# F and H projections as 2x2 block products in one list with the gates and the last projection

## The chip, the cores and the metric

The kernel runs on one core of a Trainium2 chip. The time is the device time of that core in microseconds (us), and lower is better. Before the change the median of three runs is 2470.0 us (2466.16 to 2470.41).

## What is computed

One encoder layer is applied to two sequences (batch 0 and 1) of 1024 positions with 1024 channels, all in float32. Cut to what matters here:

```python
xn = rmsnorm(x, g_pre)
p = xn @ w_in                                   # 8 sections of 1024 columns
fv, fg, hv, hg, mg = jnp.split(p, ...)
fz = jnp.fft.fftn(fv grouped, axes=(1, 3)).real # Fourier branch
y_f = (fz * jax.nn.silu(fg)) @ w_fourier_out    # the F projection
z = two long convolutions of short_conv(hv)     # Hyena branch
y_h = (z * jax.nn.silu(hg)) @ w_hyena_out       # the H projection
g_f, g_h = jnp.split(jax.nn.sigmoid(mg + b_merge), 2, axis=-1)
out = (g_f * y_f + g_h * y_h) @ w_out           # the last projection
return x + rmsnorm(out, g_post)
```

## The kernel before

Every product in float32 is made of three matmuls. A number is split into a rounded high part and the rest, both in a type that the tensor engine takes (fp32r), and `mm3` (line 369) adds high x high, high x low and low x high in one PSUM bank. `split` (line 168) is the pair of instructions that makes the parts: ACT casts the high part, and DVE (or POOL) subtracts it from the source. PE only ever sees tiles of 128x128 against 128x512.

The kernel has four phases. `phase_fourier` and `phase_main` make the Fourier branch, the filters, both convolutions and most of the gate sections; the change does not touch them. `phase_gates` and `phase_out` come last, and they are replaced.

`phase_gates` (line 971) makes the last ten pairs of gate sections of batch 1. A pair is 256 output channels by 1024 positions. It is computed as a 2x2 block product with seven multiplications in place of eight: weights and operand are cut in four blocks each, sums of blocks are formed, and `times` (line 954) runs 12 matmuls for each of seven products. `prepare` (line 981) loads the 1 MB of weights of a pair on POOL's queue, makes the sums of its blocks on DVE and splits seven operands. The operand (xn of batch 1, transposed) and the sums of its blocks are made once before the list and stay in SBUF. `first` runs the products 11 and 12 of the next pair ahead of the products s4 and 22 of the running one; `out` (line 1025) takes the four results out of PSUM, and multiplies those of two sections by a tile that it loads.

`phase_out` (line 1082) makes F and H in four units (batch, half of the positions). In a unit there are eight output tiles of F and eight of H, each of 24 matmuls of full width (`project`, line 1120): no block products. The weights of each tile are loaded on POOL's queue (`weight`, line 1106) and split, and since a unit has half of the positions they are loaded and split twice per batch. The operand of the next unit is loaded and split tile by tile beside the running one (`operand`, `rounded`, `ahead`). `gated` (line 1138) loads the merge gate, applies the sigmoid and multiplies. F stays in SBUF until H of the same tile is there, the two are added on DVE, and the sum is written to DRAM tensors `d_m`. Beside this, `beside` (line 1152) loads the last weights w_out and makes their block sums; two of the four sums are kept in DRAM (`d_t`) for a while.

`last_rows` (line 1238) makes the last projection as a list of eight pairs with the same seven products as the gates: the rows of `d_m` are the weights' side, w_out and its sums are the operand. `half_row` and `finish` do the row norm and write y.

The order of the instructions on each engine is set by a planner at compile time, from the order of the program and its own estimate of times; the queues of all engines, those of the transfers among them (SP's and POOL's), are then worked off in that order. `tc.issue_after` and `keep_in_program_order` hold single instructions back or in place.

Of the kernel before, what the change touches and what calls it, by code (L numbers as in the profile page):

```python
# [16 lines left out]
P = 128  # L17
D = 1024
# [143 lines left out]
class K:  # L162
# [34 lines left out]
    def setup(self, ctx):  # L197
# [29 lines left out]
        self.d_m = [dt(f"d_m{u}", [P, 4, 8, P]) for u in range(2 * NB)]  # L227
        self.d_t = [dt(f"d_t{j}", [P, 4, 512]) for j in range(2)]
# [734 lines left out]
    def sums(self, s, r):  # L963

        self.sub("dve", s[:, 0::2], r[:, 0:2], r[:, 1::2])
        self.stt("dve", s[:, 1], s[:, 0], -1.0, r[:, 3], MUL, SUB)
        self.add("dve", s[:, 3], s[:, 1], r[:, 2])

    PLAIN = [(5, 0), (5, 1), (6, 0), (6, 1), (5, 2), (5, 3), (6, 2), (6, 3), (5, 4), (5, 5), (6, 4), (6, 5)]

    def phase_gates(self):
# [4 lines left out]
        wp, b = self.wp, 1  # L976
        jobs = [(s, c) for c in range(0, 8, 2) for s in (0, 4, 5, 6) if (s, c) not in self.PLAIN]
        with ExitStack() as es:
            pool = lambda n: es.enter_context(tc.tile_pool(name=n, bufs=1, reuse_waits="tile"))
            gs, gw, gr = pool("gs"), pool("gw"), pool("gr")  # L980
            def prepare(sec, c):


                r = gr.tile([P, 4, 512], F32, tag="raw", name="wraw", bufs=2)
                for i in range(2):
                    nc.gpsimd.dma_start(r[:, 2 * i:2 * i + 2].rearrange("p a b -> p (a b)"), a["w_in"][sec, c + i])
                s = gw.tile([P, 4, 512], F32, tag="sum", name="wsum", bufs=1)
                A = {}

                def parts(n, pool, tags, src, bufs):  # L990
                    h, l = [pool.tile([P, 4, P], F32R, tag=t, name=t, bufs=bufs) for t in tags]
                    self.split(h.rearrange("p a b -> p (a b)"), l.rearrange("p a b -> p (a b)"), src, "dve", "act")
                    A[n] = h, l
                parts("11", wp, ("wh", "wl"), r[:, 0], 2)
                parts("12", wp, ("wh", "wl"), r[:, 1], 2)
                self.add("dve", s[:, 0:2], r[:, 2].unsqueeze(1).to_broadcast([P, 2, 512]), r[:, 3::-3])
                self.add("dve", s[:, 2], s[:, 0], r[:, 0])
# [5 lines left out]
                self.add("dve", s[:, 3], s[:, 2], r[:, 1])  # L1003
# [4 lines left out]
            A = prepare(*jobs[0])  # L1008
            TH, TL = [], []
            for k in range(4):  # L1010
                r = gr.tile([P, 4, 512], F32, tag="raw", name="xraw", bufs=2)
                for i in range(2):
                    nc.sync.dma_start(r[:, 2 * i:2 * i + 2].rearrange("p a b -> p (a b)"), self.d_x[b][k + 4 * i])
                s = gw.tile([P, 4, 512], F32, tag="sum", name="xsum", bufs=1)
                self.sums(s, r)
                h, l = [gs.tile([P, 4, 512], F32R, tag=f"{t}{k}", name=f"{t}{k}", bufs=1) for t in ("th", "tl")]
# [421 lines left out]
```

## Time and profile before

| | us |
|---|---|
| median of three runs | 2470.0 |
| lowest and highest run | 2466.16, 2470.41 |
| span of the profiled execution (first to last instruction) | 2468.1 |
| PE busy in it | 2408.3 |
| DVE busy | 1947.5 |
| ACT busy | 1093.3 |
| POOL busy | 498.2 |

The time of the profiled execution as a whole is not printed on the page; the span is what its instructions take. The page gives the busy time of each engine, and views of the trace give it for stretches of the span: PE multiplies, PEld loads PE's weights, DVE and ACT work on tiles, POOL works on tiles and issues some transfers, SP issues the others. A row of a group of instructions has the source line, the engine, the operation, output and inputs by name, their shapes, the count, busy time, the mean of one in ns, and the idle time of the engine ahead of them with what ended it. Since `split`, `tt` and `mm` are helpers, most rows carry one of their lines (171, 177, 181, 194), and the tile names tell them apart: `pin` are the products of the input projections, `pg` those of `phase_gates`, `pyf` and `pyh` those of F and H, `po` those of the last projection.

### The profile page before, as it was taken

How to read it: one execution, taken by the hardware profiler on the slowest of the kernel's cores; microseconds unless marked ns; L12 is line 12 of the kernel's file. 1: busy time of each engine (PE TensorE's matmuls, PEld its weight loads, DVE VectorE, ACT ScalarE, POOL GpSimd, SP SyncE). 2: the span in 40 equal slices, each digit the busy share in tenths (PEclk: the TensorE clock that was granted, in tenths of full speed). 3: DMA queues.
4: the chain of work that ended last, by engine and by line, in shares of the span. 5: the costliest groups of instructions: out<-in, count | busy, mean ns of one | idle time of the engine just before them, and what ended most of it. 6: DMA issues, size and time to landing. Idle time of an engine off the chain costs nothing.

```text
span 2468.1 us, 37202 instructions
## 1 busy us (share of the span) xinstructions
PE 2408.3 (98%) x13196; PEld 2090.7 (85%) x13196; DVE 1947.5 (79%) x3725; ACT 1093.3 (44%) x2041; POOL 498.2 (20%) x516
## 2 busy tenths in 40 slices
PE   6999999999989999999999999999999999999998
PEld 6988888888878988888889888888788888888886
DVE  7687788888888999999889999985565455665677
ACT  5546666666654333334223222333343444544443
POOL 1331222212234333442000000112200012112121
PEclk9999999999999999999999999999999999999999
DMA  7535544444556455545443443435445567776543
GB/s 272 180 128 210 206 163 151 156 160 156 169 184 201 161 176 175 162 161 199 137 145 129 137 144 131 136 129 175 154 162 173 196 201 267 246 244 221 165 168 128
DMA packets 225155, 429.39 MB, mean 174 GB/s; under 512 B 23542, under 2 KB 87255, under 8 KB 224456
## 3 DMA queue, kind: packets, MB, share of 16 engines
q1 hardware_dynamic: 198444, 333.34, 40.6%
q0 software_dynamic: 26336, 93.65, 10.8%
q8 instruction: 104, 1.70, 0.3%
q14 instruction: 83, 0.68, 0.1%
q10 hardware_dynamic: 188, 0.02, 0.0%
HBM read 290.60 MB, written 136.31 MB: 173 GB/s over the span
## 4 chain that ended last, share of the span: by engine, by line
PE 55%; DMA 2%; issue 1%; DVE 1%; POOL 0%; ACT 0%; DVEq 0%; SPq 0%; ACTq 0%; POOLq 0%
PE pin L194 20%; PE pg L194 8%; PE po L194 6%; PE pT L194 6%; PE pyh L194 5%; PE pX L194 5%; PE pyf L194 5%; DMA wr<-in_w_fo 1%; PE tph L785 1%; DMA g<-d_g 1%; DMA wr<-in_w_ho 0%; DVE wl L181 0%; POOL wr L1113 0%; ACT wh L171 0%; POOL wl L181 0%
## 5 line engine op out<-in xcount | busy, mean ns | idle before, releaser
L194 PE MATMUL pin<-xh,wh 128*128 128x512 f32 x1472 | 578.2, 394 | 4.3 <-DVE v L177 2.9
L194 PE MATMUL pin<-xh,wl 128*128 128x512 f32 x1472 | 577.1, 393 | 2.5 <-POOL wl L181 2.5
L194 PE MATMUL pin<-xl,wh 128*128 128x512 f32 x1472 | 578.4, 393 | 0.0
L181 POOL TENSOR_TENSOR wl<-wr,wh 128x512 fp32r<-128x512 f32 x136 | 253.5, 1865 | 1162.8 <-ACT wh L171 1120.3
L194 PEld LDWEIGHTS pin<-xh,wh 128*128 128x128 f32 x1472 | 278.4, 189 | 55.6 <-DVE v L177 3.1
L194 PEld LDWEIGHTS pin<-xh,wl 128*128 128x128 f32 x1472 | 278.3, 189 | 54.0 <-POOL wl L181 3.4
L194 PEld LDWEIGHTS pin<-xl,wh 128*128 128x128 f32 x1472 | 278.5, 189 | 51.5 <-DVE xl L181 0.4
L171 ACT CAST wh<-wr 128x512 fp32r<-128x512 f32 x264 | 162.7, 618 | 304.3 <-PE pin L194 106.8
L194 PE MATMUL pT<-cinv,yh 128*128 128x256 f32 x1024 | 192.1, 282 | 0.0
L194 PEld LDWEIGHTS pT<-cinv,yh 128*128 128x128 f32 x1024 | 164.8, 190 | 9.5 <-ACT yh L171 0.2
L181 DVE TENSOR_TENSOR t<-pX,k 128x1024 f32<-128x1024 f32 x128 | 155.4, 1214 | 9.7 <-PE pX L194 8.7
L181 DVE TENSOR_TENSOR wl<-wr,wh 128x512 fp32r<-128x512 f32 x128 | 87.1, 687 | 92.6 <-ACT wh L171 92.3
L194 PE MATMUL pX<-bh,cfwd 128*128 128x256 f32 x768 | 160.1, 287 | 0.0
L194 PE MATMUL pyf<-sf,wh 128*128 128x512 f32 x512 | 157.7, 389 | 0.0
L194 PE MATMUL pyh<-sh,wh 128*128 128x512 f32 x512 | 157.2, 389 | 0.0
L171 ACT CAST yh<-y 128x512 fp32r<-128x512 f32 x128 | 79.5, 621 | 153.7 <-DVE y L181 120.6
L194 PE MATMUL pT<-cinv,yl 128*128 128x256 f32 x512 | 144.9, 283 | 1.2 <-DVE yl L181 1.2
L171 ACT CAST bh<-b 128x512 fp32r<-128x512 f32 x144 | 88.6, 619 | 119.9 <-DVE b L181 81.5
L181 DVE TENSOR_TENSOR bl<-b,bh 128x512 fp32r<-128x512 f32 x144 | 110.6, 769 | 23.4 <-ACT bh L171 23.4
L194 PEld LDWEIGHTS pX<-bh,cfwd 128*128 128x128 f32 x768 | 125.5, 190 | 3.0
L194 PEld LDWEIGHTS pyf<-sf,wh 128*128 128x128 f32 x512 | 96.0, 188 | 20.3 <-ACT wh L171 0.5
L194 PEld LDWEIGHTS pyh<-sh,wh 128*128 128x128 f32 x512 | 96.1, 188 | 20.0
(350 smaller groups left out, 5322.9 us busy)
## 6 DMA issues: line engine op xcount, KB each, us to landing
k<-d_k SPq DMA_DIRECT2D x128, 512.0 KB, 4.0
wr<-in_w_in SPq DMA_DIRECT2D x136, 256.0 KB, 3.1
d_g<-gt SPq DMA_DIRECT2D x124, 256.0 KB, 2.5
d_k<-kt SPq DMA_DIRECT2D x128, 128.0 KB, 2.2
d_k<-kt SPq DMA_DIRECT2D x64, 256.0 KB, 2.3
wr<-in_w_fo POOLq DMA_DIRECT2D x64, 256.0 KB, 3.9
g<-d_g SPq DMA_DIRECT2D x64, 256.0 KB, 3.8
wr<-in_w_ho POOLq DMA_DIRECT2D x64, 256.0 KB, 3.8
```

The costliest lines, as they stand in the source:

```text
L171: self.rounded = nc.scalar.copy(h, src)
L181: return e.tensor_tensor(out, a, b, op=op)
L194: return self.nc.tensor.matmul(out, lhsT, rhs, start=start, stop=stop, skip_group_check=shared)
L785: nc.tensor.transpose(tp[:, q * P:(q + 1) * P], eo[:, e, q], self.ident)
```

## The change

F and H become jobs of the same list as the gates and the last projection. The new `phase_blocks` replaces `phase_gates`, `phase_out` and `last_rows`. The list is: ten gate pairs, four pairs each of F and H of batch 0, four each of F and H of batch 1, and eight pairs of the last projection. Each job has seven products of 12 matmuls. Six operands follow each other: xn of batch 1, the F operand and the H operand of batch 0, those of batch 1, and w_out.

What is new around the products:

- `staged` makes the four block sums of a coming operand on POOL, a quarter at a time: two loads on SP's queue, three POOL operations, and one store of 1 MB to `d_t` on POOL's queue. For w_out it also copies the rows to `d_wo`. It runs beside the gate jobs 1 to 8 (operands 1 and 2), the jobs 10 to 17 (operands 3 and 4) and 18 to 21 (w_out).
- Where the operand changes (the last job of each group), `room` loads and splits the blocks 00, 10 and 11 of the new operand, and `sum_of` loads and splits the four sums.
- The sums of the weights' blocks in `prepare` are on POOL for F and H, and on DVE otherwise.
- `out` of an F job writes the gated result to `d_m`; that of an H job adds its result to `d_m` in DRAM by an accumulating store on POOL's queue. `d_m` is now laid out by channel tiles, and the load for the last projection picks 128 columns of each.
- The weights of F and H are loaded and split once for each batch.
- The area for POOL's transfer descriptors is set to 8192.

The core of the diff (`last_rows` goes on as `open_row`, `half_row` and `finish` with little change):

```diff
-    def phase_gates(self):
-    def phase_out(self):
-    def last_rows(self, units, B11, B21, B22, T1, T2, T3, T4, gp, op):
+    def phase_blocks(self):
...
+        jobs = [("x", s, c) for c in range(0, 8, 2) for s in (0, 4, 5, 6) if (s, c) not in self.PLAIN]
+        for q in range(4):
+            jobs += [("fh"[q % 2], q // 2, c) for c in range(0, 8, 2)]
+        jobs += [("o", u, t) for u in range(4) for t in (0, 2)]
+        nx = len(jobs) - 24
+        operand = [0] * nx + [1 + q // 4 for q in range(16)] + [5] * 8
...
             def prepare(i):
                 kind, x, c = jobs[i]
                 r = gr.tile([P, 4, 512], F32, tag="raw", name="wraw", bufs=2)
+                for j in range(2):
+                    out = r[:, 2 * j:2 * j + 2].rearrange("p a b -> p (a b)")
+                    if kind == "o":
+                        nc.gpsimd.dma_start(out.rearrange("p (k c) -> p k c", k=8), self.d_m[x][:, :, P * (c + j):P * (c + j) + P])
+                    else:
+                        nc.gpsimd.dma_start(out, a["w_in"][x, c + j] if kind == "x" else a[f"w_{kind}o"][c + j])
                 s = gw.tile([P, 4, 512], F32, tag="sum", name="wsum", bufs=1)
+                eng = "pool" if kind in "fh" else "dve"
...
+                self.add(eng, s[:, 0:2], r[:, 2].unsqueeze(1).to_broadcast([P, 2, 512]), r[:, 3::-3])
+                self.add(eng, s[:, 2], s[:, 0], r[:, 0])
...
+                self.add(eng, s[:, 3], s[:, 2], r[:, 1])
...
+            def staged(q, k):
+                src = source(q)
+                r = ga.tile([P, 4, 512], F32, tag="draw", name="draw", bufs=1)
+                for i in range(2):
+                    nc.sync.dma_start(f2(r[:, 2 * i:2 * i + 2]), src(k + 4 * i) if q < 5 else a["w_out"][(k + 4 * i) * P:(k + 4 * i + 1) * P])
+                    if q == 5:
+                        nc.gpsimd.dma_start(src(k + 4 * i), f2(r[:, 2 * i:2 * i + 2]))
+                s = ga.tile([P, 4, 512], F32, tag="dsum", name="dsum", bufs=1)
+                self.sub("pool", s[:, 0::2], r[:, 0:2], r[:, 1::2])
+                self.sub("pool", s[:, 1], s[:, 2], r[:, 0])
+                self.add("pool", s[:, 3], s[:, 1], r[:, 2])
+                nc.gpsimd.dma_start(self.d_t[q][:, k], s)
+
+            def room(q, i, n):
+                out = []
+                for k in range(4):
+                    t = xp.tile([P, 2, 512], F32R, tag=f"x{'hl'[i - n]}{k + 4 * n}", name=f"b{i}{n}{k}", bufs=1)
+                    nc.sync.dma_start(t[:, 1].bitcast(F32), source(q)(k + 4 * i)[:, 512 * n:512 * n + 512])
+                    out.append((t[:, 0], t[:, 1]))
+                for h, l in out:
+                    self.split(h, l, l.bitcast(F32), "dve", "act")
+                return out
+
+            def sum_of(q, j):
+                h, l = t = sum_room(j)
+                nc.sync.dma_start(l.bitcast(F32), self.d_t[q][:, :, j])
+                self.split(h, l, l.bitcast(F32), "dve", "act")
+                return halves(t)
...
+            def out(i, j, n, p, q, op):
...
+                nc.sync.dma_start(f, self.d_g[x][6 if h else 5][c][:, s])
+                nc.scalar.activation(f, f, AF.Sigmoid, bias=self.bm[:, 8 * h + c:8 * h + c + 1])
                 if q is not None:
                     self.tt("dve", t, p, q, op)
+                self.mul("dve", t, p if q is None else t, f)
+                if h:
+                    nc.gpsimd.dma_start(self.d_m[2 * x + n][:, c], t, accum_op=ADD)
                 else:
+                    nc.sync.dma_start(self.d_m[2 * x + n][:, c], t)
...
+            for i, job in enumerate(jobs):
+                end = i + 1 == len(jobs)
+                turn = not end and operand[i + 1] != operand[i]
+                q = operand[min(i + 1, len(jobs) - 1)]
...
+                out(i, 0, 0, pb, m1, ADD)
+                N = dict(B)
+                if turn:
+                    N["00"], N["10"] = room(q, 0, 0), room(q, 1, 0)
+                self.times(pa, A["s2"], B[1], False)
...
+                self.times(pc, A["s3"], B[2], True)
+                self.times(pa, A["s1"], B[0], False)
...
+                if turn:
+                    for j in (1, 2, 0):
+                        N[j] = sum_of(q, j)
+                B = N
+                if not end:
+                    A = prepare(i + 1)
                     pa, pb, m1 = first(A)
...
+                self.times(pa_, A_["s4"], B_["11"], False)
+                out(i, 0, 1, pa_, None, None)
...
+                self.times(pc_, A_["22"], B_[3], False)
+                out(i, 1, 0, pc_, u, SUB)
...
+                if turn:
+                    B["11"] = room(q, 1, 1)
+                    B[3] = sum_of(q, 3)
+                for p, k in {1: (1, 0), 2: (1, 1), 3: (1, 2), 4: (1, 3), 5: (2, 0), 6: (2, 1), 7: (2, 2), 8: (2, 3)}.items() if i < nx else ():
+                    if p == i:
+                        staged(*k)
+                if nx <= i < nx + 12:
+                    staged(3 + (i - nx) // 4, (i - nx) % 4)
...
-    nc = bacc.Bacc("TRN2", target_bir_lowering=False, num_devices=1)
+    nc = bacc.Bacc("TRN2", target_bir_lowering=False, num_devices=1, dynamic_dma_scratch_size=8192)
```

More of the change, by code (lines that the diff above doesn't have):

```diff
@@ L1414, in _body @@
         k.phase_main()
[L1415 to L1416 removed]
+        k.phase_blocks()
 def kernel(**inputs):
```

432 lines of the change are left out of this document (124 added, 308 removed).

## The prediction

> **What bounds the kernel now.** I read the page first, then the chain of work in order of time over the last stages, then busy time by stage. Page, sections 0 and 1:
>
> ```profile
> span 2468.1 us, 37202 instructions
> PE 2408.3 (98%) x13196; PEld 2090.7 (85%) x13196; DVE 1947.5 (79%) x3725; ACT 1093.3 (44%) x2041; POOL 498.2 (20%) x516
> ```
>
> PE is busy in 98% of the span, but that is an average. The chain of the stages that the change touches (start, length, what):
>
> ```profile
> 1765.98 187.68 PE pg L194 x828
> 1953.66 3.17 PE pyf L194 x14
> 1956.84 2.72 PE pg L194 x12
> 1959.56 40.35 PE pyf L194 x178
> 1999.90 43.52 PE pyh L194 x192
> ...
> 2262.59 43.52 PE pyh L194 x192
> 2306.11 152.33 PE po L194 x672
> ```
>
> From 1766 to 2458 us matmuls follow each other without a gap; a 128x512 matmul costs 43.52 / 192 = 0.2267 us, in the gates (pg), in F and H (pyf, pyh) and in the last projection (po) alike. Busy time by stage (PE, PEld, DVE, ACT, POOL, clock, DMA share, GB/s), and one stretch of 16 us in which the transfers fill their engines:
>
> ```profile
> 1766.00:1959.60 193.60, 193.60 (x855) 160.30 (x855) 106.92 (x156) 77.96 (x131) 11.06 (x21) 1.00 0.47 160
> 1959.60:2306.10 346.50, 346.00 (x1523) 285.32 (x1522) 204.16 (x312) 161.41 (x266) 67.41 (x126) 1.00 0.70 235
> 2306.10:2468.10 162.00, 152.32 (x673) 125.78 (x671) 121.17 (x253) 64.93 (x134) 28.81 (x28) 0.99 0.45 148
> 2128.00:2144.00 16.00, 16.00 (x72) 13.23 (x72) 7.16 (x11) 4.96 (x9) 2.88 (x6) 1.00 1.03 357
> ```
>
> So PE alone bounds F and H (346.00 of 346.50 us, clock 1.00). The second limit is already in sight there: DMA engines 0.70 busy at 235 GB/s, and 357 GB/s is what they moved with a share of 1.03, my figure for full.
>
> **The change, part by part.** After it the list has 34 jobs: 0 to 9 the gates of batch 1 as before, then F, H of batch 0 and F, H of batch 1 with four jobs each (10 to 25), then the last projection, 26 to 33. A job is 7 products of 12 matmuls, 84 x 0.2267 = 19.04 us of PE.
>
> *Removed from PE.* F and H took 4 x 2 x 8 x 24 = 1536 matmuls; 16 jobs x 84 = 1344. 192 fewer x 0.2267 = **-43.5 us**, if PE stays as full as it is. Gates (840) and last projection (672) keep their counts.
>
> *What one F or H job puts on the other engines.* Durations from the groups of instructions:
>
> ```profile
> L181 DVE TENSOR_TENSOR wl<-wraw,wh 128x512 fp32r<-128x512 f32 x20 | 13.8, 691 | 13.0 <-ACT wh L171 13.0
> L181 DVE TENSOR_TENSOR s13l<-wsum,s13h 128x1024 fp32r<-128x1024 f32 x10 | 12.2, 1225 | 38.4 <-ACT s13h L171 38.4
> L181 DVE TENSOR_TENSOR tl<-xsum,th 128x2048 fp32r<-128x2048 f32 x4 | 9.2, 2293 | 7.9 <-ACT th L171 7.9
> L171 ACT CAST th<-xsum 128x2048 fp32r<-128x2048 f32 x4 | 7.6, 1911 | 16.4 <-DVE xsum L181 16.4
> L171 ACT CAST s13h<-wsum 128x1024 fp32r<-128x1024 f32 x9 | 9.4, 1049 | 39.1 <-PE pg L194 39.1
> L171 ACT CAST wh<-wr 128x512 fp32r<-128x512 f32 x127 | 78.2, 620 | 151.1 <-PE pyh L194 46.9 <-PE pyf L194 44.8 <-DMA wr<-in_w_fo 35.9
> L1045 ACT COPY u<-pg 128x512 f32<-128x512 f32 x10 | 5.8, 580 | 0.0
> L1143 ACT ACTIVATE g<-g,bm 128x512 f32<-128x512 f32 x64 | 46.1, 722 | 39.5 <-DMA g<-d_g 35.8 <-DVE sh L181 2.1 <-DVE wl L181 0.9
> L181 DVE TENSOR_TENSOR yf<-pyf,g 128x512 f32<-128x512 f32 x32 | 22.0, 688 | 26.0 <-PE pyf L194 22.3 <-ACT g L1143 3.7
> ```
>
> DVE per job: five splits of 512 (5 x 0.69) and one of 1024 (1.23), three sums with a PSUM tile and four gate products (7 x 0.69): 9.5 us. ACT: 5 x 0.62 + 1.05, three copies of 0.58, four sigmoids of 0.72: 8.8 us. Both lie beside 19.04 us of PE. At a **turn** (jobs 9, 13, 17, 21, 25: the next operand comes in) 12 splits of 512 (`room`) and 4 of 2048 (`sum_of`) are added: DVE 12 x 0.69 + 4 x 2.29 = 17.4 us, ACT 15.1 us.
>
> POOL's sums are new: `prepare` of F and H and every `staged` add one 1024-wide and two 512-wide operations. POOL's own times (min/median/max ns):
>
> ```profile
> L181 POOL TENSOR_TENSOR wl<-wr,wh x136: 1268/1482/7648, 194.2 to 1755.6; 128x512 fp32r<-128x512 f32 x136
> L181 POOL TENSOR_TENSOR wor<-wfv x16: 632/827/1297, 44.8 to 180.5; 128x256 f32<-128x256 f32 x16
> ```
>
> The minima double with the width, so 1024 is estimated at 2.54 us and a block of three at 2.54 + 2 x 1.27 = 5.1 us; with `staged` 10.2 us per job. By itself that is hidden, but medians lie above minima, and the timeline shows why (DVE's pieces, then POOL's, of the same time):
>
> ```profile
> 1744.22 2.29 DVE L181 TENSOR_TENSOR tl<-xsum,th 128x2048 fp32r<-128x2048 f32 x1 [1.98 <-ACT th L171]
> 1748.87 0.69 DVE L177 SCALAR_TENSOR_TENSOR xsum<-xsum,xraw 128x512 f32<-128x512 f32 x1
> 1752.26 2.29 DVE L181 TENSOR_TENSOR tl<-xsum,th 128x2048 fp32r<-128x2048 f32 x1 [1.98 <-ACT th L171]
> 1755.43 1.32 DVE L181 TENSOR_TENSOR xsum<-xraw 128x1024 f32<-128x1024 f32 x1 [0.88 <-DMA xraw<-d_x]
> 1756.79 1.66 DVE L177 SCALAR_TENSOR_TENSOR xsum<-xsum,xraw 128x512 f32<-128x512 f32 x1
> ...
> 1745.26 2.39 POOL L181 TENSOR_TENSOR wl<-wr,wh 128x512 fp32r<-128x512 f32 x1 [5.88 <-ACT wh L171]
> 1752.83 5.09 POOL L181 TENSOR_TENSOR wl<-wr,wh 128x512 fp32r<-128x512 f32 x2 [5.17 <-ACT wh L171]
> ```
>
> POOL's operation of 1745.26 ends 1.14 us after DVE's of 1744.22 ends (1746.51): it stood until then. DVE's of 1756.79, 0.69 us at 1748.87, took 1.66 and got going only when POOL's pair ended at 1757.92. Such operations exclude each other. Here all those DVE operations read two SBUF tiles. Counting only these (six splits, three gate products): 8 x 0.69 + 1.23 = 6.7 us per job, plus POOL's 10.2, plus a quarter of a turn, 4.4: 21.3 us per job with `staged`, against 19.04. [...]
>
> *What the transfers carry.* Issues (KB, median us to landing):
>
> ```profile
> wr<-in_w_fo POOLq DMA_DIRECT2D x64, 256.0 KB, 3.9
> g<-d_g SPq DMA_DIRECT2D x64, 256.0 KB, 3.8
> d_m<-yf SPq DMA_DIRECT2D x32, 256.0 KB, 4.4
> d_g<-gt SPq DMA_DIRECT2D x124, 256.0 KB, 2.5
> oraw<-in_w_out SPq DMA_DIRECT2D x8, 512.0 KB, 8.0
> t1l<-d_t SPq DMA_DIRECT2D x1, 1024.0 KB, 8.6
> ```
>
> Now weights are fetched once for each half, 128 x 0.262 = 33.6 MB; after, once for each batch, 16.8. But each job moves 1.05 MB each of weights, gates and d_m, `staged` reads 1.05 and writes 1.05 (in jobs 18 to 21 the copy of w_out adds 1.05), and a turn loads 12 x 0.262 + 4 x 1.05 = 7.3 MB. Over the 16 jobs: 50 + 30 + 4 x 7.3 = 109 MB in 305 us, 358 GB/s against 235 now and 357 when full. Between turns it is 5.25 / 19.04 = 276 GB/s (330 in jobs 18 to 21) and fits.
>
> *A turn, where it is short.* A block of the operand is free when its last product has run and wanted again 72 matmuls later (16.3 us). Behind a late `room` split stand, on the in-order DVE and ACT, the evacuations of the running job and the splits of the next `prepare`; PE waits for both; SP's queue holds gate loads and d_m stores behind loads that wait for a free tile, POOL's the next weights behind the accumulating stores, which wait for DVE's product. Over the two jobs of a middle turn (13, 17, 21), 38.1 us: transfers 2 x 5.25 + 7.3 = 17.8 MB / 357 = 49.9 us, **11.8 over**; without `staged`, which nothing needs so soon, 13.6 MB = 38.1 us, which just fits. Shared port: 2 x (6.7 + 10.2) + 17.4 = 51.2 us, 13.1 over; without `staged` 41.0, 2.9 over. Both delays lie in the same time, so the larger counts. Ends: 3 and 13; I take **8**, the middle, as `staged` is last in the program's order of a job, yet in in-order queues. Three: **+24 us**. Turn 9 has no `staged` in its first job: 2.1 + 5.25 + 7.3 = 14.7 MB = 41.1 us, 3 over. Turn 25 has none at all, 13.6 MB; but a last-projection job takes DVE 121.17 / 8 = 15.1 us: 9.5 + 15.1 + 17.4 = 42.0, 4 over. **+6 us** for the two.
>
> *Smaller parts.* (a) Batch 1's gate operand is split in 16 pieces of 512 for 4 of 2048: DVE 16 x 0.69 - 4 x 2.29 = +1.9, ACT +2.3; PE waits there already, I take +1.5. (b) The accumulating stores of H: not in the trace; nothing if they cost as a plain store (2.5 us), or their 4.2 MB once more per H group, 11.7 us; nearest to the plain rows, +1 each, +2. (c) `staged` in gate jobs 1 to 8: 5.25 MB a job, 276 GB/s; port: splits 4.7, sums 2.6, up to four gate products 2.8, POOL 5.1: 15.2 of 19.04: nothing; bound 8 x 1 us if not. (d) d_m in 512-byte pieces now moves from store (4.4 against 2.5 us) to the load for the last projection, 1.05 MB per job at 148 GB/s: hidden, 0 to 2 us. (e) POOL's smaller descriptor area: no row; I take nothing, bounds 0 and 10. (f) The end of the kernel keeps its form: nothing.
>
> **Sum:** -43.5 + 24 + 6 + 1.5 + 2 = **-10 us**. The page gives the profiled execution's span, 2468.1; its whole time is not printed; the median of the runs is 2470.0, 1.9 above the span, which I keep: **2460 us**. The measurement can tell 0.2%, 5 us, from no change.
>
> **Rivals.** *Full cover*: `staged` slips behind everything, each middle turn costs 3, the outer two 3 together: -43.5 + 9 + 3 + 3.5 = -28, 2442 us. [...] For it: 13.6 MB just fit; against: in-order queues, and the full stretch stood at 357. Chance 0.14. [...] *Break-even*: a middle turn costs its transfer price, 11.8: 35.4 + 6 + 3.5 - 43.5 = +1.4, 2471 us. For it: the 1.03 stretch shows the limit as hard. Chance 0.20. *Slower*: the two delays add instead of overlapping, because a split that came late from DMA then meets POOL's sums on the port; place: DVE in jobs 13/14, 17/18, 21/22. From 11.3 us per middle turn the gain is gone; at 16, where a third of the smaller delay is added to the larger, it is -43.5 + 48 + 6 + 3.5 = +14, 2484 us; at the full sum, 11.8 + 13.1 = 24.9, it is 2511. For it: 21.3 us of port per job are over 19.04 also without a turn's crowding. Against: DVE's 204.16 of 346.50 us leave room now. Chance 0.32. The change does remove the 192 matmuls: `times` has 12 whatever the operand; no doubt there.
>
> **How the numbers follow.** Forecast (-25 to -5) 0.34, full cover 0.14, break-even 0.20, slower 0.32. Faster by over 0.2%: 0.34 + 0.14 = 0.48; same 0.20; slower 0.32. The likeliest case's own range is 2445 to 2465; the range with 8 in 10 reaches to 2438 below, leaving part of full cover and its best bound out, and to 2492 above, leaving the far half of the adding turns.
>
> **What would show it.** 13004 matmuls; PE gaps in five places 76 us apart, released by DVE splits or DMA of `room` and `sum_of`, few elsewhere; DMA at 350 or more there; POOL sums well over 2.54 and 1.27 us, and DVE splits over 0.69, where they meet. PE gaps spread over all F and H jobs would mean the port, not the turns; gaps with DMA below 300 GB/s that the order of a queue is at fault; a longer gate stage that (c) or (e) was costed too low. I am wrong if turns cost under 3 or over 13 us each.

## The result, and the profile after

The changed kernel takes **2527.0 us** (2522.8 to 2530.0, four runs) against 2468.6 of the kernel before (2466.2 to 2470.4, four runs): a ratio of 1.0234, interval 1.0219 to 1.0249. It was forecast at 2460, with a range up to 2492. The page of the profiled execution, sections 0 and 1:

```profile
span 2528.2 us, 36972 instructions
PE 2398.2 (95%) x13004; PEld 2069.9 (82%) x13004; DVE 2083.5 (82%) x3696; ACT 1128.3 (45%) x2068; POOL 695.8 (28%) x588
```

The 192 matmuls are gone (13196 to 13004), and the span is 60.1 us longer. Busy time in three stretches (stretch, its length, PE, PEld, DVE, ACT, POOL, granted clock, DMA share, GB/s). The first is the time of the gates before, which now holds 739 of their 840 matmuls; the second, with the rest of the gates and F and H, goes on to the end of the list's last pause; the third is the rest of the last projection.

```profile
1766.00:1959.60 193.60, 172.52 (x739) 140.88 (x738) 124.69 (x136) 71.12 (x116) 79.41 (x62) 0.96 0.73 258
1959.60:2374.70 415.10, 365.42 (x1493) 291.42 (x1491) 313.33 (x304) 205.33 (x306) 191.32 (x155) 0.94 0.83 269
2374.70:2528.20 153.50, 143.82 (x623) 118.59 (x623) 125.84 (x242) 61.97 (x125) 30.43 (x27) 0.97 0.46 146
```

Before, the first of these stretches held 193.60 us of PE and F and H 346.00 of 346.50. Now PE stands idle 193.60 - 172.52 = 21.1 us in the first and 415.10 - 365.42 = 49.7 in the second. And it is slower when it works: 172.52 - 739 x 0.2267 = 5.0 us and 365.42 - 1493 x 0.2267 = 27.0 us more than the matmuls need. Together 102.8 us are lost; less the 43.5 of the removed matmuls that is +59.3, nearly the whole difference of 60.1.

**The idle part.** For each job I took the time from its first matmul to the next job's first, less 84 x 0.2267; this loss counts idle and slow time together. Summed over the records, the nine gate jobs 0 to 8 lose 26.5 us, the five turns 8.5, 10.8, 20.8, 9.6 and 12.6 (the turn's job and the next one; 62.4 together), all other jobs 17.3: some 106 us. The chain in order of time shows what stands in the gaps (start, length, what):

```profile
1808.57 9.63 DMA d_g<-gt
1818.83 2.09 DVE wsum L181
1826.88 11.03 DMA draw<-d_sh
1838.08 2.64 POOL dsum L181
...
1935.79 9.73 DMA fz<-d_g
...
2101.51 1.92 ACT th L171
2103.46 5.26 DVE tl L181
...
2166.52 20.78 DMA tl<-d_t
```

A store of a gate result, 256 KB, is 9.63 us on its way; the 41 such stores (`d_g<-gt`) after 1764 us take 7.1 us at the median, where they took 2.3 before. DVE's operations take a multiple of their time. One of the two largest gaps of the gates begins at 1814.85 and lasts 7.12 us; DVE and POOL towards its end, by the timeline:

```profile
1818.22 0.69 DVE L181 TENSOR_TENSOR gt<-pg,m 128x512 f32<-128x512 f32 x1 [7.09 <-DMA d_g<-gt]
1818.83 2.09 DVE L181 TENSOR_TENSOR wsum<-wsum,wraw 128x512 f32<-128x512 f32 x1
1820.85 1.75 DVE L181 TENSOR_TENSOR a2l<-wraw,a2h 128x512 fp32r<-128x512 f32 x1
1822.52 1.76 DVE L181 TENSOR_TENSOR gt<-gt,fz 128x512 f32<-128x512 f32 x1
...
1818.04 2.34 POOL L181 TENSOR_TENSOR dsum<-draw 128x1024 f32<-128x1024 f32 x1 [9.52 <-DMA d_t<-dsum]
1820.45 3.28 POOL L181 TENSOR_TENSOR dsum<-dsum,draw 128x512 f32<-128x512 f32 x2
```

DVE waits 7.09 us for a store to free one of three `gt` tiles; then POOL, which waited 9.52 us for its own 1 MB store, starts its three sums, and the next three DVE operations, 0.69 us each by themselves, take 2.09, 1.75 and 1.76. The operation with one input in PSUM (`gt<-pg,m`) keeps its 0.69 beside POOL's. Rows of the waits (engine and line, what it waited for: us in total, times, longest), from 1764 to 2390 us, the last two for PE alone:

```profile
POOL wsum L181 <- DVE s4l L181: 105.9, 12, 16.9
ACT fz L1115 <- DMA fz<-d_g: 73.5, 30, 7.2
...
POOL dsum L181 <- DMA d_t<-dsum: 53.4, 7, 9.7
...
PE pg L194 <- ACT u L1080: 38.7, 11, 11.5
PE pg L194 <- DVE tl L181: 18.8, 10, 3.6
```

PE itself waits for ScalarE's copy `u` of a product and for `tl`, the rounded sums of a turn.

**The slow part.** After many of the gaps PE runs at a lower granted clock for a while. The gap at 1940.79 lasts 11.63 us; the two stretches behind it:

```profile
1952.60:1956.70 4.10, 4.05 (x10) 3.24 (x11) 0.24 (x1) 0.00 (x0) 0.00 (x0) 0.53 0.86 303
1956.80:1966.90 10.10, 10.10 (x46) 8.36 (x45) 3.87 (x6) 5.22 (x9) 2.88 (x1) 1.00 1.03 403
```

Ten matmuls in 4.1 us at a clock of 0.53, then 46 in 10.1 us at 1.00. In the whole list 135 matmuls follow the one before 0.1 to 0.3 us too late, 24.7 us together; before the change there were 6. Which gaps have slow matmuls behind them is not told by their length alone, as the last section shows.

### The profile page after: what moved, and what is told of

Same layout as the page of the kernel before. It is cut to its first block, busy times and chain, and to the rows that moved or that the text cites. A ratio compares the mean times of both kernels' runs of the same rounds, so it can differ in the third digit from the quotient of the medians.

```text
span 2528.2 us, 36972 instructions
## 1 busy us (share of the span) xinstructions
PE 2398.2 (95%) x13004; PEld 2069.9 (82%) x13004; DVE 2083.5 (82%) x3696; ACT 1128.3 (45%) x2068; POOL 695.8 (28%) x588
## 4 chain that ended last, share of the span: by engine, by line
PE 36%; DMA 8%; DVE 5%; issue 3%; ACT 2%; POOL 1%; SPq 0%; DVEq 0%; ACTq 0%; POOLq 0%
PE pg L194 14%; PE pin L194 14%; PE pT L194 4%; PE pX L194 4%; DMA fz<-d_g 2%; DMA tl<-d_t 2%; DVE gt L181 1%; DVE tl L181 1%; DMA draw<-d_sh 1%; DMA xraw<-d_x 1%; DMA d_g<-gt 1%; DMA wraw<-in_w_in 1%; PE tph L786 1%; DMA b<-d_g 1%; DVE b L181 1%
## 5 line engine op out<-in xcount | busy, mean ns | idle before, releaser
L194 PE MATMUL pg<-th,s13h 128*128 128x512 f32 x272 | 114.8, 422 | 43.2 <-ACT u L1080 38.7
L171 ACT CAST wh<-wr 128x512 fp32r<-128x512 f32 x136 | 83.8, 616 | 148.2 <-PE pin L194 103.2
L194 PE MATMUL pg<-tl,s13h 128*128 128x512 f32 x272 | 114.3, 420 | 13.7 <-DVE tl L181 13.7
L194 PE MATMUL pg<-b,wh 128*128 128x512 f32 x384 | 119.6, 391 | 1.0 <-DVE b L181 1.0
L181 DVE TENSOR_TENSOR gt<-gt,fz 128x512 f32<-128x512 f32 x96 | 106.0, 1110 | 9.9 <-ACT gt L771 5.6
L194 PE MATMUL pg<-th,s13l 128*128 128x512 f32 x272 | 112.6, 414 | 0.0
```

Source lines behind the costliest of these rows:

```text
L171: self.rounded = nc.scalar.copy(h, src)
L181: return e.tensor_tensor(out, a, b, op=op)
L194: return self.nc.tensor.matmul(out, lhsT, rhs, start=start, stop=stop, skip_group_check=shared)
```

## The experiments

Times are medians; ratios are against runs of the kernel before on the same chip. The last columns are the losses of PE against 84 x 0.2267 us for each job, worked out as above. Where nothing else is said the base is the changed kernel. e1, e2, e3, e5, e6 and e10 leave out work that the layer needs (sums, stores, turns, or the addition of H to F): they price a part and are no versions of the kernel. The planner orders each program anew, so most runs differ from their base by the edit and by the order that came with it.

| run | edit | us | ratio, interval | gates | turns | other |
|---|---|---|---|---|---|---|
| changed | | 2527.0 | 1.0234 (1.0219-1.0249) | 26.5 | 62.4 | 17.3 |
| e1 | `staged` without its sums | 2497.1 | 1.0119 (1.0099-1.0140) | 7.7 | 57.9 | 9.9 |
| e2 | `staged` without its transfers | 2515.8 | 1.0196 (1.0181-1.0211) | 26.3 | 41.1 | 21.9 |
| e3 | no `staged` | 2484.9 | 1.0075 (1.0058-1.0092) | 2.3 | 37.8 | 24.5 |
| e4 | weights' sums on DVE | 2501.7 | 1.0138 (1.0123-1.0153) | 22.3 | 42.3 | 13.9 |
| e5 | e3 and e4 | 2473.4 | 1.0016 (1.0007-1.0026) | 3.3 | 29.7 | 14.8 |
| e6 | one turn of five | 2514.5 | 1.0182 (1.0167-1.0197) | 22.6 | 33.9 | 31.8 |
| e8 | all sums on DVE | 2482.9 | 1.0055 (1.0040-1.0070) | 8.8 | 45.3 | 3.8 |
| e9 | e8, `staged` not in turns | 2481.8 | 1.0051 (1.0035-1.0067) | 5.4 | 49.5 | 2.1 |
| e10 | e8, plain stores for H | 2477.2 | 1.0034 (1.0019-1.0050) | 6.7 | 41.3 | 5.3 |
| e11 | e8, staged loads on POOL's queue | 2480.7 | 1.0046 (1.0030-1.0061) | 6.9 | 38.4 | 9.7 |
| e12 | e9, gate tiles one output ahead | 2479.8 | 1.0054 (1.0035-1.0073) | 7.5 | 48.1 | 4.2 |
| e13 | e9, a turn's sums rounded later | 2481.1 | 1.0056 (1.0039-1.0073) | 7.2 | 45.0 | 4.6 |
| e14 | e13, blocks later too | 2481.7 | 1.0061 (1.0042-1.0080) | 6.7 | 43.8 | 5.6 |
| e15 | e14, sums in quarters | 2466.7 | 0.9997 (0.9987-1.0007) | 7.4 | 28.4 | 11.0 |
| e16 | changed kernel, sums in quarters | 2526.5 | 1.0227 (1.0208-1.0247) | 27.7 | 56.9 | 23.8 |
| e17 | e15, with e11 and e12 | 2468.7 | 0.9995 (0.9985-1.0006) | 9.5 | 30.1 | 8.2 |
| e18 | e14, rounded in quarters | 2479.8 | 1.0038 (1.0028-1.0049) | 6.7 | 43.6 | 7.4 |
| e19 | e14, loaded in quarters | 2485.2 | 1.0060 (1.0036-1.0084) | 7.0 | 45.9 | 11.4 |

### What does `staged` cost: its sums on POOL, or its transfers? (e1, e2, e3)

```diff
# e1
-                self.sub("pool", s[:, 0::2], r[:, 0:2], r[:, 1::2])
-                self.sub("pool", s[:, 1], s[:, 2], r[:, 0])
-                self.add("pool", s[:, 3], s[:, 1], r[:, 2])
-                nc.gpsimd.dma_start(self.d_t[q][:, k], s)
+                nc.gpsimd.dma_start(self.d_t[q][:, k], r)
# e2: the sums are made of one standing tile, nothing is loaded or stored
+                r = self.still
-                nc.gpsimd.dma_start(self.d_t[q][:, k], s)
# e3: staged does nothing; in e2 and e3 a turn loads its sums, and w_out's blocks, from tensors written long before
```

> `staged` stores the loaded blocks to d_t in place of their sums: its three POOL operations are left out, all its transfers stay. In the changed kernel (2527 us) PE loses 106 us to gaps after 1765 us: 28 in the gate jobs, 62 in the two jobs of each turn, 17 elsewhere. Transfers theory (the megabytes of `staged` stand ahead of small loads and stores that in-order engines wait for): within 8 us of 2527. Port theory (POOL's sums and DVE's two-tile operations exclude each other): 25 to 40 us less, near 2495, with the gate jobs losing under 10.

> `staged` makes its three POOL operations on a tile that stays in place, and neither loads nor stores; the turns load as many bytes as before, from tensors that are written earlier, so values are not the reference's. Transfers theory: 50 to 75 us less than 2527, near 2465, gate jobs losing under 5. Port theory: within 15 us of 2527. Turn theory (what is short is the turn's own 7.3 MB and 16 splits in 38 us): gate jobs lose little, turns keep over 45 of their 62 us, total near 2490.

> `staged` is left out whole (turns load as many bytes from other tensors). What is left over the full gain (2425 + 5) is due to the turns, the port use of the weights' sums and the jobs themselves. Transfers theory: the same as without the transfers alone, within 8 us of it. Port theory: the same as without POOL's sums alone. Both together: lower than either by 10 or more; if turns cost what I predicted without `staged`, 3 us each, near 2445; turn theory: still 2480 or more.

Without POOL's sums the kernel is 30 us faster, without the transfers 11, without both 42: the two add. In the gates it is the sums: 26.5 us of loss fall to 7.7 without them and stay at 26.3 without transfers. That these two figures are equal is partly chance. In e2 nothing holds POOL's sums back, so the 60 of them ran in one go from 1748 to 1893 us, 106.7 us of them in jobs 0 to 8 in place of 63.8, and the loss lies in pieces of 1 to 7 us in jobs 0 to 5, where the changed kernel has 9.4 in job 2 and 13.5 in job 8. What both have is DVE held up: added over its operations in jobs 0 to 8, the time above the shortest of their kind is 31.6 us in the changed kernel, 63.3 in e2, 1.9 in e1, and 1.4 in e8, where DVE makes the sums itself.

A rival for the gates is POOL's queue, which also issues the weight loads: in the changed kernel POOL stands 89 us there (1764 to 1960 us) before staged operations that wait for a transfer. But in e1 it stands 77 us and the gates lose 7.7, and in e2 none and they lose 26.3. In the two long gaps of the changed kernel DVE waits 7.1 and 7.6 us for a store of `gt` ahead of its slowed operations; how these late stores hang together with the sums is not shown. The transfers show at the turns: 62.4 to 41.1.

### The other sums on POOL (e4, e5), and all of them on DVE (e8)

```diff
# e4
-                eng = "pool" if kind in "fh" else "dve"
+                eng = "dve"
# e8: besides, in staged
-                self.sub("pool", s[:, 0::2], r[:, 0:2], r[:, 1::2])
+                self.sub("dve", s[:, 0::2], r[:, 0:2], r[:, 1::2])
...
```

> The block sums of the weights of F and H are on DVE, as they are in the gates, and POOL keeps those of `staged` alone; nothing is left out. Port theory: 2.6 us of DVE for 5.1 of POOL in each of 16 jobs, 10 to 25 us less, 2502 to 2517. Transfers theory: within 8 us of 2527. Turn theory: DVE has 2.6 us more per job at a turn where it is the last in line, 0 to 15 us more.

> `staged` is left out whole (the turns load as many bytes from other tensors) and the block sums of F's and H's weights are on DVE, so POOL makes no sums at all until the last projection. Port theory: the two gains add, 2485 - 25 = 2460, and what stays is the turns' own price, 25 to 40 us over the full gain. Rival, that the weights' sums helped only because POOL was crowded by `staged`: 2475 to 2490.

> The sums of `staged` and of the weights of F and H are all on DVE (nothing is left out): 2.6 us of DVE for 5.1 of POOL each. Port theory: less load on the shared port than with the weights' sums alone on DVE, but it is all DVE's now; gate jobs lose under 8 instead of 27, total 2480 to 2500. DVE-capacity rival: 9.5 + 2.6 + 2.6 + 4.4 = 19.1 us per job against 19.04, F and H jobs lose more, 2505 to 2530.

The same work on DVE is 44 us cheaper than on POOL (2527.0 to 2482.9), though DVE is the busier engine by far. With the weights' sums alone on DVE (e4) the kernel gains 25 us, and with `staged` gone as well (e5) 54, between the two theories: the gains of 42 (e3) and 25 do not add to 67, so in part they are the same. POOL's sums by tile in the changed kernel (count, min/median/max ns, first and last start):

```profile
L181 POOL TENSOR_TENSOR wsum<-wsum,wraw x32: 1281/1604/2754, 1971.4 to 2326.6; 128x512 f32<-128x512 f32 x32
L181 POOL TENSOR_TENSOR wsum<-wraw x16: 2367/2410/3323, 1967.0 to 2320.0; 128x1024 f32<-128x1024 f32 x16
L181 POOL TENSOR_TENSOR dsum<-dsum,draw x40: 1282/1622/1844, 1750.6 to 2172.8; 128x512 f32<-128x512 f32 x40
L181 POOL TENSOR_TENSOR dsum<-draw x20: 2334/2481/3079, 1748.1 to 2166.9; 128x1024 f32<-128x1024 f32 x20
```

and DVE's gate product with two SBUF inputs, the first row of the changed kernel, the second of e8; the third is the operation with one input in PSUM, of the changed kernel again:

```profile
L181 DVE TENSOR_TENSOR gt<-gt,fz x80: 676/691/6641, 1774.2 to 2371.7; 128x512 f32<-128x512 f32 x80
L181 DVE TENSOR_TENSOR gt<-gt,fz x80: 677/683/695, 1778.4 to 2324.9; 128x512 f32<-128x512 f32 x80
L181 DVE TENSOR_TENSOR gt<-pg,m x52: 673/681/693, 1771.2 to 2356.4; 128x512 f32<-128x512 f32 x52
```

An operation of 0.69 us that stands up to 6.64 us beside POOL's sums never exceeds 0.695 without them: of the 80 in the first row 26 take over 0.75 us, and each of these has a sum of POOL beside it for 0.84 us or more. The one with a PSUM input never exceeds 0.693, though 16 of its 52 have a sum of POOL beside them for over 0.3 us. The prediction's estimates of POOL's durations (2.54 and 1.27 us) were near: medians 2.41 to 2.48 and 1.60 to 1.62. What it took for a share of a 19.04 us budget held up single operations of DVE, up to 6.64 us for 0.69, and behind them what stands in DVE's queue, PE's next operand (`tl`) included. For the weights' sums a second way is open: a block of three takes 2.41 + 2 x 1.60 = 5.6 us on POOL and some 2.6 on DVE, and ScalarE waits 24.5 us for them in 12 places (`s2h`); how much of e4's 25 us is this delay and how much the hold-up of DVE was not separated.

### Are the turns dear by themselves? (e6)

```diff
-                turn = not end and operand[i + 1] != operand[i]
+                turn = not end and operand[i + 1] != operand[i] and operand[i] == 0
```

> Four of the five turns (jobs 13, 17, 21, 25) are left out: F and H of all batches and the last projection multiply the operand that the first turn brought; `staged` and everything else stay. Turn theory: the four segments lose 54 us now and keep at most 10, so 2527 - 45 = 2482 or less. Port theory: the splits of a turn are a fifth of the port's load in those jobs (4.4 of 21.3 us), so other jobs gain too, 2470 to 2482. If turns only collect delays that would fall elsewhere: 2500 or more, with the jobs between them losing more than now.

Four of five turns taken out gain only 12 us. The jobs at which these four stood still lose 26.9 of their 53.8 us (33.9 with the turn that stays), and the others lose more than before (31.8 for 17.3). About half of what shows at the turns is therefore not of the turns' own making: with the work of the turns gone, delays come to PE there and elsewhere. That POOL's sums make most of these fits e8 (45.3 us at the turns for 62.4) but is not shown by this run alone.

### With the sums on DVE, 58 us of loss are left. Staging, stores, queue, gate loads? (e9 to e12)

```diff
# e9 on e8: twelve staged blocks in jobs 10, 11, 12, 14, 15, 16, 18, 19, 20, 22, 23, 24
-                if nx <= i < nx + 12:
-                    staged(3 + (i - nx) // 4, (i - nx) % 4)
+                place = {10: 0, 11: 1, 12: 2, 14: 3, ..., 24: 11}.get(i)
+                if place is not None:
+                    staged(3 + place // 4, place % 4)
# e10 on e8
-                    nc.gpsimd.dma_start(self.d_m[2 * x + n][:, c], t, accum_op=ADD)
+                    nc.gpsimd.dma_start(self.d_m[2 * x + n][:, c], t)
# e11 on e8, for q1 to q4 and w_out
-                    nc.sync.dma_start(f2(r[:, 2 * i:2 * i + 2]), src(k + 4 * i) if q < 5 else ...
+                    nc.gpsimd.dma_start(f2(r[:, 2 * i:2 * i + 2]), src(k + 4 * i) if q < 5 else ...
# e12 on e9: out() takes a gate tile fz that was asked for at the output before
+                f = ahead.pop((i, j, n), None)
+                ask(turns.index((i, j, n)) + 1)
```

> On top of all sums on VectorE (2482.9 us). The twelve staged blocks of q3 to q5 go to jobs 10, 11, 12, 14, 15, 16, 18, 19, 20, 22, 23, 24, so that no job with a turn stages any. Transfers theory (with the sums off GpSimd the transfers are the bound at the turns: DMA share 1.00 at 361 GB/s from 2032 to 2108 us; a block is 2 MB, 3 MB for w_out, so 6 to 9 us of transfers leave each of the turns at 13, 17 and 21): these turns fall from 10.8, 5.4 and 6.2 us to under 4 each, the time to 2465 to 2472. Rival (what is left at the turns is the order of one engine's work, not transfers): the turns stay, 2480 to 2486.

> On top of all sums on VectorE (2482.9 us). H's 32 stores are plain stores: H is not added to F, the rest is as before. Theory (an accumulating store costs only its issue on GpSimd and some reading beside, 0 to 2 us on the end, term (b) of the prediction): 2480 to 2485. Rival (the accumulating stores hold up GpSimd's queue of weight loads and add reads to a full DMA, worth 8 us or more): under 2475, with less loss in the H jobs 14 to 17 and 22 to 25.

> On top of all sums on VectorE (2482.9 us). The staged blocks of q1 to q4 are loaded from GpSimd's queue in place of SP's, where the small loads and stores of the outputs (256 KB) go. Theory of the queue (256 KB transfers wait behind 1 MB of staged loads on their own queue; fz<-d_g landed in 5.9 us, tl<-d_t in 12): the median landing of fz falls under 5 us and the time by 4 to 10 us, to 2473 to 2479. Rival (the 16 DMA engines are shared whatever the queue): same within 2 us. It could also be slower, over 2486, if a block's load waits for its tile on GpSimd's queue and holds the weights' loads behind it.

> On top of e9 (no staging in the turns' jobs): each load of a gate tile fz is issued one output earlier, so that ScalarE does not stand before Sigmoid and hold up the copies m and u behind it (ACT fz waited 56 us for DMA fz<-d_g between 1955 and 2400 us with all sums on VectorE, 73 us in the changed kernel). Theory (ScalarE's wait in order is what is left): that wait falls under 20 us and the time by 5 to 12 us below e9, below the kernel before (2468) if e9 gives 2465 to 2472. Rival (the wait is slack; TensorE has 4.2 us of matmuls in hand): within 2 us of e9.

**e9 tried nothing.** The row of the staged stores in e8 and then in e9 (first and last start):

```profile
L1039 POOL DMA_DIRECT2D d_t<-dsum x20: 534/539/579, 1753.0 to 2098.9; - x20
L1039 POOL DMA_DIRECT2D d_t<-dsum x20: 534/539/579, 1748.6 to 2093.5; - x20
```

The last staged store is issued in job 15 in both kernels (at 2093.5 us in e9), although e9's program has its last block in job 24. The planner issues a staged block as soon as it can, wherever the program has it, and the engines got the same order. In the changed kernel it had done the same: the 20 stores start in jobs -1 (ahead of the list), 0, 1, 2, 2, 3, 4, 5, 6, 7, 8, 8, 9, 10, 11, 12, 13, 16, 17 and 18, where the prediction had counted 1 to 8 and 10 to 21. Whether blocks that are really held away from the turns would help was not tried.

Plain stores (e10) gain some 5 us on e8; the intervals overlap, so this is a size, not a proof. The queue (e11) is worth nothing that can be told: the turn at job 9 falls from 11.1 us to 2.1 and that at 17 rises from 5.4 to 11.9, so the loss moves, and the sum of all losses nearly stays (57.9 and 55.0).

**e12 tried nothing either.** In its trace SP's transfers come in the order of e9's but for 4 of 1180 places, and a load of a merge gate is issued 7.8 us before its sigmoid at the median in both. The planner had already asked for each tile two gate products ahead in e9, as soon as one of the three `fz` tiles was free. Whether earlier gate loads would help stays open. It takes more tiles: a kernel with six (e7, on e5) has no time, since the last projection's pool needs 14.6 KB per partition and 10.6 are left.

### The order of the engines, or the landing of the sums? (e13 to e16, e18, e19)

```diff
# e13 on e9
                 if turn:
-                    for j in (1, 2, 0):
-                        N[j] = sum_of(q, j)
+                    late = [(j, sum_load(q, j)) for j in (1, 2, 0)]
-                B = N
                 if not end:
                     A = prepare(i + 1)
+                if turn:
+                    for j, t in late:
+                        N[j] = sum_split(t)
+                B = N
# e14 on e13: the rounding of room's blocks 00 and 10 behind u = kept(pa, True)
# e15 on e14 (e16: the same in the changed kernel; e18 only the rounding, e19 only the loads)
-                nc.sync.dma_start(t[1].bitcast(F32), self.d_t[q][:, :, j])
+                for k in range(4):
+                    nc.sync.dma_start(t[1][:, k].bitcast(F32), self.d_t[q][:, k, j])
...
-                self.split(h, l, l.bitcast(F32), "dve", "act")
+                for k in range(4):
+                    self.split(h[:, k], l[:, k], l[:, k].bitcast(F32), "dve", "act")
```

> On top of e9 (2481.8 us; losses at the turns 11.0, 13.1, 5.3, 7.6, 12.6). The loads of a turn's three sums are issued where they were, their rounding (th on ScalarE, tl on VectorE) behind the work on the next job's weights instead of ahead of it. Theory (engines' order: ScalarE stands 5 us before th for DMA tl<-d_t, VectorE 2.5 us behind it, and the next weights' copies and m and u queue behind): ScalarE's wait for tl<-d_t goes from 26 us under 8, the turns from 49.5 to 25 to 38, the time to 2465 to 2475. Rival (TensorE needs T1 at a time that only the landing sets): within 3 us of e9, as TensorE then waits for th and tl instead.

> On top of e13: the rounding of a turn's first two blocks of B (eight tiles b) comes behind the copy u instead of ahead of it. Theory of the order: the waits of TensorE for ScalarE's u (37 us in e9 with the weight loads' share) fall under 15 us and the time by 3 to 10 us more, to 2458 to 2470. Rival (landing): the stall only changes place, to TensorE waiting for b, within 3 us of e13.

> On top of e14: each 1 MB load of a sum is four of 256 KB, each rounded as it lands. Theory of the landing (12 us for 1 MB plus 1.9 and 2.3 us of rounding stand against some 16 us from the last use of the old sum to the first use of the new): the first quarter is ready 5 to 8 us earlier, and the time falls by 4 to 12 us below e14. Theory of the order, if it has taken all: within 2 us of e14, or 2 to 4 us over it for 60 more instructions on ScalarE and VectorE each and 60 more on SP.

e13 and e14 did not reach the engines either. ScalarE at the first turn, in e9 and then in e14:

```profile
1981.04 1.91 ACT L171 CAST th<-tl 128x2048 fp32r<-128x2048 f32 x1 [4.92 <-DMA tl<-d_t]
1982.84 1.05 ACT L171 CAST s13h<-wsum 128x1024 fp32r<-128x1024 f32 x1
```

```profile
1981.11 1.91 ACT L171 CAST th<-tl 128x2048 fp32r<-128x2048 f32 x1 [4.96 <-DMA tl<-d_t]
1982.92 1.04 ACT L171 CAST s13h<-wsum 128x1024 fp32r<-128x1024 f32 x1
```

In the traces of e8, e9, e13 and e14 all instructions of ScalarE, VectorE, SP and GpSimd come in the same order by operation and tile name, so these are one kernel four times over: 2482.9, 2481.8, 2481.1 and 2481.7 us. Their misses say nothing of the order of the engines; they say how well the medians repeat.

e15 is 15 us faster than that and level with the kernel before. PE's waits from 1764 to 2370 us, e14 and then e15:

```profile
PE pg L194 <- ACT u L1094: 16.5, 10, 3.6
PE pg L194 <- DVE tl L181: 14.5, 7, 2.8
```

```profile
PE pg L194 <- ACT u L1096: 19.1, 11, 5.1
PE pg L194 <- DVE tl L181: 1.5, 4, 0.6
```

The wait for the rounded sums is gone. The first turn, e14 and then e15:

```profile
1960.00:1986.00 26.00, 20.14 (x73) 15.42 (x72) 19.52 (x22) 13.89 (x18) 1.59 (x3) 0.87 0.90 350
```

```profile
1960.00:1986.00 26.00, 25.14 (x106) 19.34 (x105) 23.23 (x37) 17.17 (x31) 1.59 (x3) 1.00 0.87 321
```

106 matmuls run in the time of 73, at a mean granted clock of 1.00 in place of 0.87.

> The changed kernel (2527.0 us) with one edit: the sums of a turn come in four loads of 256 KB and are rounded in quarters; all sums stay on GpSimd. Theory A (the landing of a 1 MB sum costs its own 15 us, as between e14 and e15): 2508 to 2516. Theory B (with the sums on GpSimd the turns wait for slowed VectorE work, and an earlier landing has nothing to win): 2522 to 2530, or more, as 60 more VectorE instructions each meet GpSimd's sums.

> On top of e14 (2481.7 us): one 1 MB load of each sum, as there, but rounded in quarters; e15 (2466.7) has both. Theory of the rounding (a whole cast of 1.9 us and a whole subtraction of 2.3 us stand between the landing and the first matmul, a quarter's 0.6 and 0.7 would do: 2.9 us for each of five turns, and shorter pieces let copies of u and m in between): most of the 15 us, 2466 to 2472. Theory of the landing: 2478 to 2483.

> On top of e14 (2481.7 us): four 256 KB loads of each sum, but one rounding of the whole. Theory of the rounding: 2479 to 2484, as e14. Theory of the landing (256 KB landed in 7.8 us at the median where 1 MB took 12.4): 2466 to 2475.

Neither half does it: rounding in quarters alone gains 2 us (up to 6 by the ratios, with overlapping intervals), loads in quarters alone lose 3, so both theories, that of the rounding and that of the landing, fall as they stood. A sum has to pass a load (12.4 us for 1 MB in e14, 7.8 for a quarter in e15, medians), a cast of 1.9 and a subtraction of 2.3 between the last use of its tile and the next, 72 matmuls or 16.3 us later. Only when a quarter can be rounded while the next one lands does the chain fit. That the two together work by this overlap is my reading; the runs show only that neither edit alone has the gain. The order of the engines changed with each edit (in e18, which leaves SP's program as it was, 36 of SP's 1180 transfers stand in another place), and losses moved: four turns of e18 lose 29.3 us in place of 38.3 in e14, and that at job 17 loses 14.3 in place of 5.5. So what a half is worth in an unchanged order is open. In the changed kernel quarters gain nothing (e16); that POOL's sums hold the same splits back first would explain it, and was not tested.

### The next bound (e17)

> On top of e15 (2466.7 us): gate tiles one output ahead (as e12) and staged blocks loaded from GpSimd's queue (as e11). Theory (once the sums land in time, what stands before u is next: ScalarE waits 78 us for DMA fz<-d_g, TensorE 44 us for u with the weight loads' share): 2454 to 2462, faster than the kernel before. Rival (VectorE's backlog sets u: the old u is released by DVE gt, and VectorE has no idle time between 2043 and 2061 us): within 3 us of e15.

Level with e15, and with the kernel before. The time is the rival's, but the theory was hardly tried: as in e12, the gate loads did not move (7.1 us before the sigmoid at the median in both e15 and e17), so of the two edits only the queue did anything. In e15 the copy `u` has this row; the last two lines say what its engine idled for:

```profile
L1096 ACT COPY u<-pg x30: 567/582/589, 1773.3 to 2368.5; 128x512 f32<-128x512 f32 x30
its engine sat idle before it (us, times) until:
  DVE gt L181: 6.4, 9
  PE pg L194: 4.2, 4
```

`u` has one buffer, and DVE's product `gt<-pg,u` releases it. That DVE, which has taken over POOL's sums, releases it late at the turns is a reading of this row. A second buffer for `u` was not tried. No version was faster than the kernel before; e15 and e17 equal it.

## Why the prediction was wrong, step by step

- **The bound and the 43.5 us: right.** 13004 matmuls; PE was the bound, and every microsecond lost on it came out at the end (102.8 - 43.5 = 59.3 against 60.1).
- **(c) `staged` in gate jobs, "nothing": the step that failed first.** It was weighed as an average, 15.2 us of DVE's and POOL's work, added up as if they exclude each other, in jobs of 19.04, with a bound of 8. Gates lost 26.5, and 7.7 without POOL's sums (e1). The average hid how far a single wait goes (DVE's operations of jobs 0 to 8 were held up 31.6 us, and they stand in order in front of PE's evacuations), and the count of blocks was wrong as well: the planner issued eleven staged stores in jobs 0 to 8, and one ahead of them, where I had eight. The prediction puts such work down to a shared port, and counts for DVE its operations with two SBUF inputs alone: 6.7 us a job in the 51.2 us of a turn, from which the upper end of 13 comes. No run shows a port, nor that this count is right; they show `gt<-gt,fz` at up to 6.64 us beside POOL's sums and at most 0.695 without them (e8), and `gt<-pg,m` at most 0.693 beside them.
- **The turns, +24 and +6: mis-sized by half.** 62.4 us in place of 30, with 20.8 at the worst where my upper end was 13. The named places were right. But POOL's sums are 17 us of them (45.3 in e8), and the 1 MB sums' chain of load and rounding another 15 (43.8 in e14, 28.4 in e15). The prediction saw the 16.3 us of room for a block, and did not add up what has to fit into them.
- **"The larger delay counts": wrong.** Sums 30, transfers 11, both 42 (e1 to e3), and at the turns alone 4.5, 21.3 and 24.6: the delays add. That is what the rival "slower" said; its reason, a late split that then meets POOL's sums, is not shown by itself, its place was too narrow, since it named the turns only, and at its full price of 24.9 us per turn it ended at 2511. (Its middle case has a slip: a third of 11.8 on top of 13.1 is 17.0 per turn, not 16, and 2487.)
- **"Between turns ... fits": wrong,** 17.3 us, with the sums on DVE 3.8 (e8), without the transfers 21.9 (e2): POOL again, not the transfers.
- **No term for the clock.** Many of the gaps were followed by a stretch at a lower granted clock (4.1 us at 0.53 in the row above), and the late matmuls are 24.7 us in sum. The rows of before hold no such gap in the stages that I looked at, and I priced a gap at its length.
- **The figure for full transfers, 357 GB/s, was low for a short stretch** (403 GB/s at a share of 1.03, in the row above), and right for a long one: 361 GB/s over 57 us of the second turn.

```profile
2051.00:2108.00 57.00, 47.10 (x186) 36.26 (x184) 50.71 (x45) 33.40 (x48) 26.13 (x22) 0.94 1.00 361
```

- **Small terms.** (a) and (e): the list of jobs starts at 1764.9 us after 1765.8 before, so nothing was lost ahead of it, and (a)'s 1.5 us was not paid. (b): 2 us taken, some 5 measured (e10), in its bounds. (d), (f): the last projection has no gaps; nothing, as taken.
- **The signs did their work.** "PE gaps spread over all F and H jobs would mean the port", "a longer gate stage that (c) or (e) was costed too low": both came.

## What to carry to other kernels

Work that is moved to an idle engine is not free if its operations and those of a busy engine hold each other up, as POOL's sums and DVE's operations with two SBUF inputs do here (up to 6.64 us for 0.69): ask what the busy engine's next instruction holds up, not what share of the time is left. Where an operand is replaced in place, add up the chain from the last use to the next (load, cast, subtraction) and cut load and rounding in the same pieces. Look at the order that a planner emitted before reading a run that moved lines: three of these runs (e9, e13, e14) moved nothing, and the gate loads of two more (e12, e17) did not move.

## What the runs showed of the hardware

- The length of a gap of PE did not tell alone whether the granted clock fell. After one of 2.06 us at 2281.08 four us at 0.59 follow (first two rows), after one of 2.89 us at 2040.49 four us at 1.00 (last two rows). Of the 28 gaps of 0.6 us or more in the changed kernel's list, the six of over 3 us were all followed by slow matmuls, the eight of under 1.6 us by none (two late ones at the most), and those between went both ways. What tells the two gaps below apart was not tried.

```profile
2281.30:2283.30 2.00, 0.17 (x1) 0.00 (x0) 2.00 (x2) 0.72 (x1) 1.99 (x3) 1.00 1.03 324
2283.40:2287.40 4.00, 4.00 (x11) 3.21 (x12) 4.00 (x4) 0.62 (x1) 2.66 (x2) 0.59 0.87 302
...
2040.70:2043.50 2.80, 0.18 (x1) 0.00 (x0) 2.80 (x3) 1.05 (x3) 2.72 (x3) 1.00 0.00 0
2043.50:2047.50 4.00, 3.90 (x17) 3.21 (x18) 4.00 (x2) 1.40 (x3) 3.98 (x4) 1.00 0.71 162
```

- Where the planner mixed a sigmoid of F with the last Silu of the gates, ScalarE loaded a table three times within 5.3 us, 1.28 us each, in the middle of PE's longest gap (11.63 us):

```profile
1945.61 1.28 ACT L1115 ACT_TABLE_LOAD   x1 [9.39 <-DMA fz<-d_g]
1946.90 0.72 ACT L1115 ACTIVATE fz<-fz,bm 128x512 f32<-128x512 f32 x1
1947.64 1.28 ACT L1107 ACT_TABLE_LOAD   x1
1948.94 0.63 ACT L1107 ACTIVATE gt<-gt 128x512 f32<-128x512 f32 x1
1949.59 1.28 ACT L1115 ACT_TABLE_LOAD   x1
```
